# Norm 2 of an encoder layer: four differences go from GpSimd to VectorE, and VectorE's block gets an order of its own

## The chip, the core and the metric

The kernel runs on one core of a Trainium2 chip. The metric is the time of one execution on the device in microseconds. TensorE (PE in the profile) multiplies, VectorE (DVE), ScalarE (ACT) and GpSimd (POOL) work on elements, SyncE (SP) issues the transfers. Each engine works off its own queue in order; semaphores tie the queues together.

## The reference

One encoder layer on 1024 positions of 1024 features, in float32. This is the part that matters here, the second half of the layer:

```python
def rmsnorm(x, g):
    y = x32 * lax.rsqrt(jnp.mean(x32 * x32, axis=-1, keepdims=True) + RMS_EPS)
    return (y * g.astype(jnp.float32)).astype(x.dtype)
...
x = x + gate1 * (merged @ w_out[i])
h2 = rmsnorm(x, g_ffn[i]) * (1 + scale2) + shift2
u = depthwise_conv_seq(h2 @ w_up[i], conv_w[i], conv_b[i])
u_val, u_gate = jnp.split(u, 2, axis=-1)
x = x + gate2 * ((jax.nn.gelu(u_gate, approximate=True) * u_val) @ w_down[i])
```

Before it come the projections, two kinds of attention and the gates; after it a last norm. `w_up` has 1024 x 5632 elements.

## The kernel before

**Precision.** Every product of float32 matrices is three matmuls of a reduced type: each operand is split into a rounded part and the rest (`hi` by ScalarE, `lo = x - hi` by VectorE or GpSimd), and high x high, high x low and low x high are added up in one PSUM bank (lines 948 to 950 for the products of this stage).

**Seven products for eight.** `h2 @ w_up` is done in 22 tiles of 128 columns of each of the two halves of u. Each tile is one 2 x 2 block product by a scheme of seven block products: the weights give the operands 11, S2, S1, S3, 12, S4 and 22, the data give B11, T2, T1, T3, B21, B22 and T4. Positions fall into two halves, features into rows of 128. With B11 and B21 the first four and last four feature rows of half 0 of h2, B12 and B22 those of half 1, the data operands are T3 = B22 - B12, T2 = B11 + T3, T1 = B22 - T2 and T4 = B21 - T2, four rows of 128 x 512 each. They are made once, at norm 2, and serve all 22 tiles.

**The norm 2 block.** `m1[0..7]` are the rows of half 0 (tiles `big` in the profile), scaled and split long before. `m2[0..7]` are those of half 1 (`x` in the profile, x_8576, x_8612, x_8650, x_8688 for 0 to 3 and x_8730, x_8769, x_8808, x_8849 for 4 to 7 in the queues). As soon as the rows come out of the w_out product, `m2[k]` for k < 4 is replaced by the difference `m2[k+4] - m2[k]`: GpSimd makes the first three (line 1123), VectorE the last (line 1129). The reciprocal root of the mean square (`rs`: VectorE line 98, ScalarE line 99, VectorE line 100) is spread over the partitions by TensorE into the PSUM bank `pbc` (line 106). Then VectorE scales the eight rows with it (line 1210), makes `t2[0..3]` = T2 (line 1212; tiles `big` and `wc`) and T1 (line 1214, into `big`). `shifted` (1068 on ScalarE, 1069 on VectorE) adds the shift and splits T2, T3 and B22; `operand` (894 on ScalarE, 895) splits T1 on VectorE and T4 on GpSimd. GpSimd makes T4 (line 1221) between its weight splits (line 56).

**Orders.** Most of the program is put in order by a scheduler that models times. Within the block a written order holds on ScalarE, VectorE and GpSimd, and TensorE's order is as written from the last w_out product to the end of the block. TensorE begins tiles 0 and 1 before the norm is there, with B11 and B21, and goes on with T2, T1, T3, B22 and T4 as they come. What drains the banks of a tile are lines 954 (ScalarE), 956, 958, 961, 966 and 970 (VectorE), the convolution lines 1138 (ScalarE) and 1144 (VectorE), then 1170 (gelu) and 1171. `a_operands` prepares the weights of the next tile: GpSimd 912 to 914, VectorE 921, and splits whose `hi` is ScalarE's line 55 (`whi`, `wsh`, `big`) and whose `lo` is GpSimd's line 56 (`wlo`, `wsl`, `big`). Loads of `w_up` (line 1096, into `wraw` and `big`) start when the tile they fill comes free.

Of the kernel before, what the change touches and what calls it, by code (L numbers as in the profile page):

```python
# [12 lines left out]
OP = mybir.AluOpType  # L13
# [15 lines left out]
def hybrid_encoder(tc, xT, c, w_ada, small, w_in, p1_bias, p23_bias, na_bias, ln2_mult, ident, w_br, w_out,  # L29
                   w_up, w_down, out):  # L30
    nc = tc.nc
    act, dve, pool, pe, sp = nc.scalar, nc.vector, nc.gpsimd, nc.tensor, nc.sync
# [5 lines left out]
    def f(ap):  # L38
        return ap.bitcast(FT)
# [56 lines left out]
    def rstd_of(pcol, n):  # L96
        r = wpool.tile([128, KT], FT, name="rs", bufs=2)
        dve.tensor_scalar(r[:, :n], pcol[:, :n], 1.0 / D, EPS, OP.mult, OP.add)
        act.activation(r[:, :n], r[:, :n], AF.Sqrt)
        dve.reciprocal(r[:, :n], r[:, :n])  # L100
        return r

    def bcast(r, psum_pool, tag, n=4):
        pb = psum_pool.tile([128, 512], FT, name="pbc", tag=tag)
        for t in range(n):
            pe.transpose(pb[:, t * 128:(t + 1) * 128], r[:, t:t + 1].to_broadcast([128, 128]), idt)
        return pb
# [688 lines left out]
    def half_tile(dtype=FT):  # L796
        return mxpool.tile([128, 512], dtype, name="x2", bufs=16)
# [95 lines left out]
    def operand(t, hi, lo, lo_eng):  # L893
        act.activation(hi, t, AF.Copy)
        lo_eng.tensor_tensor(lo, t, f(hi), OP.subtract)
# [85 lines left out]
    def wide(dtype=FT):  # L981
        return keep.tile([128, 512], dtype, name="wc", bufs=5)

    def big(shape, dtype=FT):
        return keep.tile(shape, dtype, name="big", bufs=9)
# [81 lines left out]
    def shifted(src, b, hi, lo):  # L1067
        act.activation(hi, src, AF.Identity, bias=b)
        dve.scalar_tensor_tensor(lo, src, b, f(hi), OP.add, OP.subtract)

    def out_tile(hf, m, sqa, scaled):

        cols = halves[hf]
        w = out_w.pop()
        if hf + m < KT:
            out_w.append(w_split(w_load(w_out[(m + 1) % KT]), pool))
        p = ps.tile([128, 512], FT, name="pj", bufs=6)
        product(p, w, lambda k: [t[:, k, cols] for t in ms])
        xx = x2[hf][m]
        dve.scalar_tensor_tensor(xx, p, ada[:, 16 + m:17 + m], xx, OP.mult, OP.add)  # L1080
        sp.dma_start(x_scr[m][:, cols], xx)
# [19 lines left out]
    m1 = [raw[k // 2][:, k % 2] for k in range(KT)]  # L1101
# [7 lines left out]
    bc = bcast(rstd_of(pcol, 4), ps, "pbc")  # L1109
# [5 lines left out]
    m2 = []  # L1115
# [10 lines left out]
    late_mm.enter_context(tc.manual_schedule(engines={pe.engine}))  # L1126
    m2.append(half_tile())
    sq = out_tile(1, KT - 1, sqa, m2[KT - 1])
    dve.tensor_tensor(m2[3], m2[7], m2[3], OP.subtract)
    mpool.release()  # L1130
    oppool2 = tc.alloc_tile_pool(name="ops2", bufs=1, side="right", reuse_waits="tile")
    for n in ("T2", "T1", "T3"):
# [3 lines left out]
    with tc.tile_pool(name="up", bufs=2, reuse_waits="tile") as work:  # L1136
# [58 lines left out]
        bc = bcast(rstd_of(pcol, 4), ps, "pbc")  # L1195
# [4 lines left out]
        t2 = big([128, 2, 512])  # L1200
        t2 = [t2[:, 0], t2[:, 1], wide(), wide()]

        def t_split(n, k, src, b):
            shifted(src, b, ops[n][0][:, k], ops[n][1][:, k])

        with tc.manual_schedule(engines={act.engine, dve.engine, pool.engine}):

            for k in range(10):
                if k < 8:
                    dve.tensor_tensor(m2[k], m2[k], bc, OP.mult)  # L1210
                if 1 <= k < 5:
                    dve.tensor_tensor(t2[k - 1], m2[k - 1], m1[k - 1], OP.add)
                elif k >= 5 and k < 9:
                    dve.tensor_tensor(m1[k - 5], m2[k - 1], t2[k - 5], OP.subtract)  # L1214
                if 2 <= k < 6:
                    t_split("T2", k - 2, t2[k - 2], shift2[:, 2 + k:3 + k])
                elif k >= 6:
                    operand(m1[k - 6], ops["T1"][0][:, k - 6], ops["T1"][1][:, k - 6], dve)
            for k in range(4):
                t_split("T3", k, m2[k], dshift[:, k:k + 1])  # L1220
                pool.tensor_tensor(m1[4 + k], m1[4 + k], t2[k], OP.subtract)
            for k in range(4):
                late["B22"].append((half_tile(FR), half_tile(FR)))
                shifted(m2[4 + k], shift2[:, 4 + k:5 + k], *late["B22"][k])
            for k in range(4):
                late["T4"].append((half_tile(FR), half_tile(FR)))
                operand(m1[4 + k], *late["T4"][k], pool)
        for g in gens:
# [81 lines left out]
    with tc.manual_schedule(engines={dve.engine}):  # L1310
# [28 lines left out]
        hf, cs, bc = before  # L1339
# [118 lines left out]
```

## Time and profile before

| | |
|---|---|
| three runs | 1565.9, 1569.3 and 1570.37 us; median 1569.3 us |
| the profiled execution | 1566.2 us; its span 1564.4 us; mean granted clock 0.982 |
| busy | PE 96%, PEld 83%, DVE 65%, ACT 52%, POOL 51% |
| the norm 2 block | about 884 to 925 us of the span |
| the 22 tiles of w_up | about 881 us to 1320 us |

A row of the timeline gives the start and the length in microseconds, the engine, the line, the operation, what it writes and reads, and in brackets how long the engine had stood idle before and which engine ended that. The length of a row counts from when the engine took the instruction up, so time in which it is held up by something other than a semaphore is in its length. Rows that follow each other on one line are merged, with a count.

### The profile page before, as it was taken

How to read it: one execution, taken by the hardware profiler on the slowest of the kernel's cores; microseconds unless marked ns; L12 is line 12 of the kernel's file. 1: busy time of each engine (PE TensorE's matmuls, PEld its weight loads, DVE VectorE, ACT ScalarE, POOL GpSimd, SP SyncE). 2: the span in 40 equal slices, each digit the busy share in tenths (PEclk: the TensorE clock that was granted, in tenths of full speed). 3: DMA queues.
4: the chain of work that ended last, by engine and by line, in shares of the span. 5: the costliest groups of instructions: out<-in, count | busy, mean ns of one | idle time of the engine just before them, and what ended most of it. 6: DMA issues, size and time to landing. Idle time of an engine off the chain costs nothing. (4 is left out here: it accounts for less than half of the span.)

```text
span 1564.4 us, 22094 instructions
## 1 busy us (share of the span) xinstructions
PE 1509.5 (96%) x8012; PEld 1291.5 (83%) x8012; DVE 1024.4 (65%) x1874; ACT 805.8 (52%) x1448; POOL 801.8 (51%) x500
## 2 busy tenths in 40 slices
PE   8999799999999999999999888999999999999998
PEld 7899788888887998888888767888888887788787
DVE  6686266676756665535625888766666667877775
ACT  4432366666766677643335454444444446575542
POOL 1242243444337566411256858666666665679621
PEclk9899899999999999999999999999999999999999
DMA  9458522223133453557734212322222223533313
GB/s 352 164 201 292 156 73 73 81 77 93 51 90 111 141 138 104 184 187 238 228 128 149 74 54 81 108 81 81 81 82 90 86 74 136 182 114 121 115 54 109
DMA packets 114421, 196.87 MB, mean 126 GB/s; under 512 B 40200, under 2 KB 61576, under 8 KB 114312
## 3 DMA queue, kind: packets, MB, share of 16 engines
q1 hardware_dynamic: 114040, 195.20, 38.0%
q8 instruction: 63, 1.03, 0.3%
q14 instruction: 46, 0.38, 0.1%
q10 hardware_dynamic: 272, 0.26, 0.1%
HBM read 158.73 MB, written 42.47 MB: 129 GB/s over the span
## 5 line engine op out<-in xcount | busy, mean ns | idle before, releaser
L56 POOL TENSOR_TENSOR wlo<-wraw,whi 128x1024 fp32r<-128x1024 f32 (+2 forms) x78 | 179.9, 2307 | 284.1 <-ACT whi L55 275.1
L79 PE MATMUL pj<-h,whi 128*128 128x512 f32 x448 | 180.5, 403 | 3.8 <-ACT h L202 2.2
L80 PE MATMUL pj<-h,whi 128*128 128x512 f32 x448 | 179.4, 400 | 0.3 <-DVE h L204 0.3
L81 PE MATMUL pj<-h,wlo 128*128 128x512 f32 x448 | 178.8, 399 | 0.0
L56 POOL TENSOR_TENSOR wsl<-big,wsh 128x1024 fp32r<-128x1024 f32 (+1 forms) x45 | 109.3, 2432 | 50.6 <-ACT wsh L55 50.6
L1144 DVE SCALAR_TENSOR_TENSOR big<-wc,sm,big 128x256 f32<-128x256 f32 (+1 forms) x132 | 115.0, 919 | 17.3 <-ACT big L1138 17.2
L55 ACT ACTIVATE whi<-wraw 128x1024 fp32r<-128x1024 f32 (+2 forms) x81 | 81.3, 1003 | 87.0 <-PE pj L80 25.9
L338 POOL TENSOR_SCALAR kl<-kl 64x512 fp32r<-64x512 f32 x32 | 63.8, 1994 | 80.4 <-DVE kl L336 78.1
L79 PEld LDWEIGHTS pj<-h,whi 128*128 128x128 f32 x448 | 85.3, 190 | 20.6 <-ACT ks L337 3.4
L80 PEld LDWEIGHTS pj<-h,whi 128*128 128x128 f32 x448 | 85.4, 191 | 15.9 <-DVE h L204 1.1
L81 PEld LDWEIGHTS pj<-h,wlo 128*128 128x128 f32 x448 | 85.2, 190 | 15.0
L575 DVE CUSTOM_DVE_ANT_0 P<-S,bias 128x256 f32<-128x256 f32 x128 | 52.3, 420 | 53.7 <-PE S L622 31.9
L576 ACT ACTIVATE P<-P,st 128x256 f32<-128x256 f32 x128 | 64.3, 503 | 39.3 <-DVE st L575 38.7
L1144 DVE SCALAR_TENSOR_TENSOR big<-pj,sm,big 128x512 f32<-128x512 f32 x132 | 67.9, 564 | 16.1 <-ACT big L1138 16.1
L56 POOL TENSOR_TENSOR wsl<-wraw,wsh 128x768 fp32r<-128x768 f32 (+1 forms) x23 | 50.1, 2178 | 47.7 <-ACT wsh L55 47.7
L1138 ACT ACTIVATE big<-wc,sm 128x512 f32<-128x512 f32 x44 | 35.8, 816 | 74.5 <-DVE wc L961 45.6
L239 PE MATMUL pv<-vwh,h 128*128 128x256 f32 x256 | 73.7, 288 | 0.4 <-ACT vs L246 0.4
L240 PE MATMUL pv<-vwl,h 128*128 128x256 f32 x256 | 72.5, 283 | 0.0
L241 PE MATMUL pv<-vwh,h 128*128 128x256 f32 x256 | 72.5, 283 | 0.0
L527 POOL TENSOR_TENSOR vv<-vv 96x256 fp32r<-96x256 f32 (+2 forms) x32 | 41.0, 1294 | 59.3 <-ACT vv L526 59.1
L55 ACT ACTIVATE wsh<-big 128x1024 fp32r<-128x1024 f32 (+1 forms) x45 | 44.9, 1002 | 35.4 <-POOL big L913 18.3
L1170 ACT ACTIVATE big<-big 128x1024 f32<-128x1024 f32 x22 | 23.3, 1060 | 76.6 <-DVE big L1144 76.6
(379 smaller groups left out, 4923.7 us busy)
## 6 DMA issues: line engine op xcount, KB each, us to landing
wraw<-w_in SPq DMA_DIRECT2D x36, 512.0 KB, 3.5
wada<-w_ada SPq DMA_DIRECT2D x31, 512.0 KB, 7.1
big<-w_up SPq DMA_DIRECT2D x22, 512.0 KB, 5.0
wraw<-w_up SPq DMA_DIRECT2D x22, 512.0 KB, 3.7
as<-big SPq DMA_DIRECT2D x22, 512.0 KB, 3.0
big<-as SPq DMA_DIRECT2D x22, 512.0 KB, 8.1
wraw<-w_down SPq DMA_DIRECT2D x24, 384.0 KB, 4.2
gs<-gs SPq DMA_DIRECT2D x32, 256.0 KB, 2.5
```

The costliest lines, as they stand in the source:

```text
L55: act.activation(hi, raw, AF.Copy)
L56: lo_eng.tensor_tensor(lo, raw, f(hi), OP.subtract)
L79: pe.matmul(psum, whi[:, k0 + k], mhi, start=k == 0, stop=False)
L80: pe.matmul(psum, whi[:, k0 + k], mlo, start=False, stop=False)
L81: pe.matmul(psum, wlo[:, k0 + k], mhi, start=False, stop=k == n - 1)
L239: pe.matmul(p, hhi, hi[:, k], start=fresh and k == 0, stop=False, skip_group_check=True)
L240: pe.matmul(p, hhi, lo[:, k], start=False, stop=False, skip_group_check=True)
L241: pe.matmul(p, hlo, hi[:, k], start=False, stop=k == KT - 1, skip_group_check=True)
L338: pool.tensor_scalar(ll[b], f(ll[a]), 1.0, None, OP.mult)
L575: dve.tensor_tensor_reduce(pp, d, bias, -1.0, BIG, OP.add, OP.min, mi)
L576: act.activation(pp, pp, AF.Exp, bias=mi, scale=-1.0, accum_out=li)
L1144: dve.scalar_tensor_tensor(y[:, dst], src, wt, y[:, dst], OP.mult, OP.add)
```

## The change

The fourth difference of `m2` no longer stands ahead of the reciprocal. It is made inside the block, of rows 3 and 7 that have both been scaled, where before the difference of the unscaled rows was scaled afterwards. The loop of the block is written out in an order of its own. The four differences of T4 go from GpSimd, where they stood beside the T3 splits, to VectorE, after the splits of B22 and each just ahead of its own T4 split.

```diff
     sq = out_tile(1, KT - 1, sqa, m2[KT - 1])
-    dve.tensor_tensor(m2[3], m2[7], m2[3], OP.subtract)
...
-            for k in range(10):
-                if k < 8:
-                    dve.tensor_tensor(m2[k], m2[k], bc, OP.mult)
-                if 1 <= k < 5:
-                    dve.tensor_tensor(t2[k - 1], m2[k - 1], m1[k - 1], OP.add)
-                elif k >= 5 and k < 9:
-                    dve.tensor_tensor(m1[k - 5], m2[k - 1], t2[k - 5], OP.subtract)
-                if 2 <= k < 6:
-                    t_split("T2", k - 2, t2[k - 2], shift2[:, 2 + k:3 + k])
-                elif k >= 6:
-                    operand(m1[k - 6], ops["T1"][0][:, k - 6], ops["T1"][1][:, k - 6], dve)
...
+            scale(0)
+            scale(1)
+            t2_sum(0)
+            scale(2)
+            t2_sum(1)
+            t2_split(0)
+            scale(7)
+            scale(3)
+            t2_split(1)
+            t2_sum(2)
+            dve.tensor_tensor(m2[3], m2[7], m2[3], OP.subtract)
+            t2_split(2)
+            t2_sum(3)
+            scale(4)
+            t2_split(3)
+            t1_sum(0)
...
             for k in range(4):
                 t_split("T3", k, m2[k], dshift[:, k:k + 1])
-                pool.tensor_tensor(m1[4 + k], m1[4 + k], t2[k], OP.subtract)
...
             for k in range(4):
+                dve.tensor_tensor(m1[4 + k], m1[4 + k], t2[k], OP.subtract)
                 late["T4"].append((half_tile(FR), half_tile(FR)))
                 operand(m1[4 + k], *late["T4"][k], pool)
```

`scale`, `t2_sum`, `t1_sum` and the two splits are the same operations as in the loop, given names. Lines move: scaling is line 1208, T2's sums 1211, T1's 1217, the moved difference 1231, T4's differences 1252; from the convolution to the gelu lines are one lower (1137, 1143, 1169).

VectorE's queue at the start of the block, before (pcol and rs are the sums and the reciprocal root, pbc the spread of it):

```order
L98 TENSOR_SCALAR rs<-pcol 128x4
L1129 TENSOR_TENSOR x_8688<-x_8849,x_8688 128x512
L100 RECIPROCAL rs<-rs 128x4
L1210 TENSOR_TENSOR x_8576<-x_8576,pbc 128x512
L1210 TENSOR_TENSOR x_8612<-x_8612,pbc 128x512
L1212 TENSOR_TENSOR big<-x_8576,big 128x512
L1210 TENSOR_TENSOR x_8650<-x_8650,pbc 128x512
L1212 TENSOR_TENSOR big<-x_8612,big 128x512
L1069 SCALAR_TENSOR_TENSOR T2lo<-big,ada,T2hi 128x512
L1210 TENSOR_TENSOR x_8688<-x_8688,pbc 128x512
```

and the same place now:

```order
L98 TENSOR_SCALAR rs<-pcol 128x4
L100 RECIPROCAL rs<-rs 128x4
L1208 TENSOR_TENSOR x_8576<-x_8576,pbc 128x512
L1208 TENSOR_TENSOR x_8612<-x_8612,pbc 128x512
L1211 TENSOR_TENSOR big<-x_8576,big 128x512
L1208 TENSOR_TENSOR x_8650<-x_8650,pbc 128x512
L1211 TENSOR_TENSOR big<-x_8612,big 128x512
L1069 SCALAR_TENSOR_TENSOR T2lo<-big,ada,T2hi 128x512
L1208 TENSOR_TENSOR x_8849<-x_8849,pbc 128x512
L1208 TENSOR_TENSOR x_8688<-x_8688,pbc 128x512
L1069 SCALAR_TENSOR_TENSOR T2lo<-big,ada,T2hi 128x512
L1211 TENSOR_TENSOR wc<-x_8650,big 128x512
```

The difference of rows 3 and 7 (x_8688, x_8849) no longer stands between line 98 and the reciprocal; row 7 is scaled among the first rows instead of last.

VectorE's queue at the end of the block, before (x_9053 to x_9065 are the low parts of B22):

```order
L1069 SCALAR_TENSOR_TENSOR x_9053<-x_8730,ada,x_9052 128x512
L1069 SCALAR_TENSOR_TENSOR x_9057<-x_8769,ada,x_9056 128x512
L958 TENSOR_TENSOR wc<-pj,wc 128x512
L1069 SCALAR_TENSOR_TENSOR x_9061<-x_8808,ada,x_9060 128x512
L958 TENSOR_TENSOR wc<-pj,wc 128x512
L1069 SCALAR_TENSOR_TENSOR x_9065<-x_8849,ada,x_9064 128x512
L961 TENSOR_TENSOR wc<-pj,wc 128x512
```

and now (the low parts of B22 are x_9049 to x_9061):

```order
L1069 SCALAR_TENSOR_TENSOR x_9049<-x_8730,ada,x_9048 128x512
L1069 SCALAR_TENSOR_TENSOR x_9053<-x_8769,ada,x_9052 128x512
L958 TENSOR_TENSOR wc<-pj,wc 128x512
L1069 SCALAR_TENSOR_TENSOR x_9057<-x_8808,ada,x_9056 128x512
L1069 SCALAR_TENSOR_TENSOR x_9061<-x_8849,ada,x_9060 128x512
L1252 TENSOR_TENSOR big<-big 128x512 x2
L1252 TENSOR_TENSOR big<-big,wc 128x512 x2
L961 TENSOR_TENSOR wc<-pj,wc 128x512
L958 TENSOR_TENSOR wc<-pj,wc 128x512
```

The four differences stand ahead of line 961 of tile 0 and line 958 of tile 1, which drain banks. On GpSimd the four rows of line 1221 that stood between the three `wsl` splits and the split of `big` are gone and nothing takes their place.

TensorE's queue at the first products of tile 2, before:

```order
L948 MATMUL pj<-B21hi,whi 128x512
L949 MATMUL pj<-B21lo,whi 128x512
L950 MATMUL pj<-B21hi,wlo 128x512
L948 MATMUL pj<-T2hi,wsh 128x512
L949 MATMUL pj<-T2lo,wsh 128x512
L948 MATMUL pj<-T1hi,wsh 128x512
L949 MATMUL pj<-T1lo,wsh 128x512
L948 MATMUL pj<-T3hi,wsh 128x512
```

and now:

```order
L948 MATMUL pj<-B11hi,whi 128x512
L949 MATMUL pj<-B11lo,whi 128x512
L950 MATMUL pj<-B11hi,wlo 128x512
L948 MATMUL pj<-T2hi,wsh 128x512
L949 MATMUL pj<-T2lo,wsh 128x512
L948 MATMUL pj<-T1hi,wsh 128x512
L949 MATMUL pj<-T1lo,wsh 128x512
L948 MATMUL pj<-B21hi,whi 128x512
```

The scheduler now puts tile 2's first T2 and T1 matmuls ahead of its twelve B21 matmuls; T3's come after those as before. The orders of tiles 0 to 4 differ in such places, up to where tile 5's first matmuls stand; from there to the end of w_up the products of both kernels stand in the same order.

More of the change, by code (lines that the diff above doesn't have):

```diff
@@ L1206, in hybrid_encoder, with scale, t2_sum, t2_split @@
         with tc.manual_schedule(engines={act.engine, dve.engine, pool.engine}):
-            for k in range(10):
-                if k < 8:
-                    dve.tensor_tensor(m2[k], m2[k], bc, OP.mult)
-                if 1 <= k < 5:
-                    dve.tensor_tensor(t2[k - 1], m2[k - 1], m1[k - 1], OP.add)
-                elif k >= 5 and k < 9:
-                    dve.tensor_tensor(m1[k - 5], m2[k - 1], t2[k - 5], OP.subtract)
-                if 2 <= k < 6:
-                    t_split("T2", k - 2, t2[k - 2], shift2[:, 2 + k:3 + k])
-                elif k >= 6:
-                    operand(m1[k - 6], ops["T1"][0][:, k - 6], ops["T1"][1][:, k - 6], dve)
+            def scale(k):
+                dve.tensor_tensor(m2[k], m2[k], bc, OP.mult)
+            def t2_sum(k):
+                dve.tensor_tensor(t2[k], m2[k], m1[k], OP.add)
+            def t2_split(k):
+                t_split("T2", k, t2[k], shift2[:, 4 + k:5 + k])
+            def t1_sum(k):
+                dve.tensor_tensor(m1[k], m2[4 + k], t2[k], OP.subtract)
+            def t1_split(k):
+                operand(m1[k], ops["T1"][0][:, k], ops["T1"][1][:, k], dve)
+            scale(0)
[14 more added lines that the diff above has]
+            t1_sum(0)
+            scale(5)
+            t1_sum(1)
+            t1_split(0)
+            scale(6)
+            t1_split(1)
+            t1_sum(2)
+            t1_sum(3)
+            t1_split(2)
+            t1_split(3)
             for k in range(4):
                 t_split("T3", k, m2[k], dshift[:, k:k + 1])
-                pool.tensor_tensor(m1[4 + k], m1[4 + k], t2[k], OP.subtract)
             for k in range(4):
```

## The prediction, made before the changed kernel was run

> **What bounds the kernel now.** I read the page first, then TensorE's timeline around norm 2, the table by stretches, then the timelines of the three other engines there.
>
> ```profile
> PE 1509.5 (96%) x8012; PEld 1291.5 (83%) x8012; DVE 1024.4 (65%) x1874; ACT 805.8 (52%) x1448; POOL 801.8 (51%) x500
> 887.01 0.62 PE L106 MATMUL pbc<-idt,rs 128*128 128x128 f32 x4 [4.27 <-DVE rs L100]
> 902.22 0.51 PE L949 MATMUL pj<-T2lo,wsh 128*128 128x512 f32 x1 [2.41 <-DVE T2lo L1069]
> 910.39 0.50 PE L949 MATMUL pj<-T1lo,wsh 128*128 128x512 f32 x1 [3.01 <-DVE T1lo L895]
> 951.60 0.50 PE L948 MATMUL pj<-B21hi,whi 128*128 128x512 f32 x1 [2.65 <-ACT wc L954]
> 975.30 0.50 PE L948 MATMUL pj<-x,big 128*128 128x512 f32 x1 [1.81 <-DVE wc L958]
> ```
>
> TensorE bounds the kernel. Between 880 and 1000 us it stands still for over 1 us five times, 14.15 us in all, and these are the only stalls the change can reach: three wait for VectorE inside the block, two come after it, in tiles 3 and 4.
>
> ```profile
> 880.00:890.00 10.00, 5.73 (x26) 4.48 (x26) 9.11 (x10) 3.41 (x6) 10.00 (x5) 0.89 0.03 10
> 900.00:910.00 10.00, 5.17 (x21) 3.79 (x21) 10.00 (x12) 3.67 (x6) 4.28 (x2) 1.00 0.15 52
> 910.00:920.00 10.00, 9.61 (x35) 7.76 (x36) 8.96 (x12) 7.33 (x12) 3.13 (x2) 0.83 0.01 2
> 920.00:930.00 10.00, 10.00 (x46) 8.28 (x45) 6.71 (x12) 2.12 (x3) 8.99 (x7) 1.00 0.44 157
> 950.00:960.00 10.00, 8.40 (x30) 6.77 (x31) 6.67 (x7) 7.61 (x10) 7.43 (x3) 0.83 0.48 159
> 970.00:980.00 10.00, 8.19 (x30) 6.24 (x29) 7.75 (x8) 3.54 (x5) 6.94 (x5) 0.83 0.20 63
> ...
> 888.79 0.63 PE L949 MATMUL pj<-B11lo,whi 128*128 128x512 f32 x1
> 889.22 0.63 PE L950 MATMUL pj<-B11hi,wlo 128*128 128x512 f32 x1
> ...
> 893.41 0.39 PE L949 MATMUL pj<-B21lo,whi 128*128 128x512 f32 x1
> 893.64 0.39 PE L950 MATMUL pj<-B21hi,wlo 128*128 128x512 f32 x1
> ```
>
> The third figure from the end is the granted clock. A share of 0.83 over 10 us is 3.4 us at half speed. There matmuls follow each other every 0.43 us instead of 0.23, so a half-clock stretch costs 3.4 x (1 - 0.23/0.43) = 1.6 us. Four of the five stalls brought one, the one of 2.41 us (900 to 910, clock 1.00) did not.
>
> **VectorE's chain through the block.**
>
> ```profile
> 883.95 0.15 DVE L98 TENSOR_SCALAR rs<-pcol 128x4 f32<-128x4 f32 x1
> 884.02 2.75 DVE L1129 TENSOR_TENSOR x<-x,x 128x512 f32<-128x512 f32 x1
> 886.70 0.16 DVE L100 RECIPROCAL rs<-rs 128x4 f32<-128x4 f32 x1
> 887.67 1.29 DVE L1210 TENSOR_TENSOR x<-x,pbc 128x512 f32<-128x512 f32 x2 [0.80 <-PE pbc L106]
> ...
> 890.07 2.27 DVE L1212 TENSOR_TENSOR big<-x,big 128x512 f32<-128x512 f32 x1
> 892.26 1.79 DVE L1069 SCALAR_TENSOR_TENSOR T2lo<-big,ada,T2hi 128x512 fp32r<-128x512 f32 x1
> ...
> 898.05 0.74 DVE L1069 SCALAR_TENSOR_TENSOR T2lo<-wc,ada,T2hi 128x512 fp32r<-128x512 f32 x1
> 898.71 0.68 DVE L1210 TENSOR_TENSOR x<-x,pbc 128x512 f32<-128x512 f32 x1
> ...
> 900.41 1.75 DVE L1069 SCALAR_TENSOR_TENSOR T2lo<-wc,ada,T2hi 128x512 fp32r<-128x512 f32 x1
> ...
> 906.28 2.85 DVE L1214 TENSOR_TENSOR big<-x,wc 128x512 f32<-128x512 f32 x1
> ...
> 909.66 1.28 DVE L895 TENSOR_TENSOR T1lo<-big,T1hi 128x512 fp32r<-128x512 f32 x2
> 884.13 0.20 ACT L99 ACTIVATE rs<-rs 128x4 f32<-128x4 f32 x1 [1.82 <-DVE rs L98]
> 883.44 8.35 POOL L56 TENSOR_TENSOR wsl<-big,wsh 128x1024 fp32r<-128x1024 f32 x3
> 891.75 3.45 POOL L1221 TENSOR_TENSOR big<-big 128x512 f32<-128x512 f32 x2
> 899.89 1.72 POOL L56 TENSOR_TENSOR big<-wraw,big 128x512 fp32r<-128x512 f32 x1
> 905.92 2.67 POOL L56 TENSOR_TENSOR wlo<-wraw,whi 128x1024 fp32r<-128x1024 f32 x1 [4.30 <-ACT whi L55]
> ```
>
> A pass that reads one operand from PSUM takes 0.60 us (two in 1.29, the second 0.69 long) whatever GpSimd does. One that reads two from SBUF takes the same when GpSimd is idle, but ends only 0.6 us after a running GpSimd instruction does: the sum at 890.07 ends at 892.34, the three `wsl` splits at 891.79. So VectorE queues behind GpSimd instruction by instruction. Three splits less two VectorE passes of 0.6 that got in between, from 884.0 to 891.79, make 2.2 us a split. A T2 low part costs 0.66 (898.05 to 898.71).
>
> **The change, step by step.** *The difference ahead of the reciprocal.* The root is there at 884.33; the reciprocal comes at 886.70, since L1129 stood behind a `wsl` split. Without it the reciprocal starts at about 884.4: 2.3 us earlier, and TensorE's first stall shrinks from 4.27 to 1.95. Scaling begins at 885.35.
>
> *GpSimd takes most of that back.* The first T2 sum, at 886.55, meets the second split (886.2 to 888.4) and ends at 889.0. The second waits out the third split and ends at 891.8, 0.5 us ahead of before.
>
> *The four differences leave GpSimd.* The first low part of T2 then need not wait for line 1221 (892.26, 1.79 long): it ends at 892.5 instead of 894.05. Two scalings and the second low part: 894.35.
>
> ```profile
> 896.42 0.76 ACT L1138 ACTIVATE big<-pj,sm 128x512 f32<-128x512 f32 x1
> 897.08 0.62 ACT L55 ACTIVATE big<-wraw 128x512 fp32r<-128x512 f32 x1
> 898.16 0.72 ACT L1068 ACTIVATE T2hi<-wc,ada 128x512 fp32r<-128x512 f32 x1 [0.46 <-DVE wc L1212]
> 904.78 1.06 ACT L55 ACTIVATE whi<-wraw 128x1024 fp32r<-128x1024 f32 x1 [0.75 <-DMA wraw<-w_up]
> 901.64 18.30 SPq L1096 DMA_DIRECT2D wraw<-w_up  x2
> ```
>
> ScalarE now does the convolution and the split of `big` (0.76 and 0.62) right after the second T2 high part, at 892.5, so GpSimd's split of `big` gets in behind the second low part, 894.35 to 895.6, and holds up the third T2 sum to 896.2. The moved difference (0.6) to 896.8, then the low part once its high part (0.72) is there, 897.7; the fourth sum and one scaling; the last low part ends at 899.75 against 902.16. The load of `w_up` is issued when that split ends, 895.6 instead of 901.6, and lands 3.1 us later (901.64 to 904.78); ScalarE takes it at 899.05, and GpSimd's `wlo` split holds the port from 900.35 to 902.55, where it held it at 906.28 before. It costs VectorE one wait of 1 us, not 2.2: the second T1 sum ends at 903.15. Seven passes of 0.6 later, at 907.4, stands the third low part of T1, for which TensorE waited before (909.66 + 0.68 = 910.34). **TensorE is then 2.9 us ahead.** If the `wlo` split held up two passes, not one, it would be 1.9; if none, 3.9.
>
> *The differences on VectorE.* Four passes, 2.4 us, more where one meets a T4 split. VectorE is 6.71 busy of 10 between 920 and 930, which hides them from TensorE's T4 products. But they stand ahead of lines 961, 958 and 966, and ScalarE's convolution and the weight splits of tile 2 stand behind those.
>
> ```profile
> 937.54 1.04 ACT L55 ACTIVATE wsh<-wraw 128x1024 fp32r<-128x1024 f32 x1
> ...
> 938.74 0.40 PE L948 MATMUL pj<-T3hi,wsh 128*128 128x512 f32 x1
> ```
>
> Before, that split of tile 2 was done at 938.58, 0.16 us ahead of its first use. With TensorE 2.9 us ahead and ScalarE held by 2.4 us of differences, the split comes 0.5 us ahead of before, and TensorE waits there for 2.9 - 0.16 - 0.5 = 2.2 us. Bounds: 0 (the differences fit into VectorE's idle time) and 5 (they don't, and a T4 split is waited for twice).
>
> *The later stalls.* Those at 951.60 and 975.30 hang on the drain of tiles 2 and 3, whose order is new too. I take them as they are, 4.46 us, give or take 1.5. The few swaps in the w_down stage I cost at nothing, give or take 1: no stall of the block reaches them.
>
> *The clock.* TensorE's waits become more and shorter. By the rows, 1.81 us is enough for a half-clock stretch and 2.41 may do without, so I count half a stretch fewer than the four: -0.8; bounds -3.2 and +1.6. The Trainium skill (TensorE: Matmul & The Clock Gate, Part 1) lets the clock fall only after an idle window of about 3.4 us; by that the 4.27 us stall alone was charged, and with 1.95 us its 1.6 us would go for certain. The trace disagrees: 0.83 at 970 to 980 follows a stall of 1.81.
>
> **The sum.** -2.9 + 2.2 + 0 - 0.8 = -1.5 us. The profiled execution took 1566.2 us (span 1564.4 and 1.8 around it) and lies at the low end of the runs (1565.9 to 1570.37); set against the median of 1569.3 it gives **1567.8 us**, 0.1% less. A measurement of this kernel can tell about 0.3%, 4.7 us, from no change.
>
> **Rivals.** *VectorE becomes the bound behind the block* (slower). The four differences, each behind a GpSimd instruction, put the drains of tiles 0 and 1 so late that tile 2's splits come later than the 937.54 of before; that is the point from which it decides. TensorE then waits the whole 2.9 in tile 2 and the 2.4 of the differences on top, and two more half-clock stretches come: -2.9 + 5.3 + 3.2 = +5.6, 1574.9 us. For it: VectorE is 8.96 and 10.00 busy of 10 just before. Against it: 6.71 after, with idle time before the drains.
>
> *The whole advance is kept* (faster). Tile 2 does not wait, since ScalarE's splits come as early as TensorE, and two half-clock stretches go: -2.9 - 3.2 = -6.1, 1563.2 us. For it: the head stall of 1.95 and a broken T1 wait may both keep the clock. Against it: the slack of 0.16 us before that split's use.
>
> *The moved difference gains nothing* (no change): GpSimd's three splits end at the same time either way and T2's sums wait for them. Then 0.5 us of the advance is left, and with the tile 2 wait gone too and the clock as it is, -0.5: 1568.8 us. It shares its class with the forecast.
>
> **Chances.** Forecast 0.50 and no gain 0.14, both within 0.3%: 0.64. Whole advance kept 0.20, VectorE the bound 0.16. The range is 1563.0 to 1574.0: the forecast with the bounds of the T1 wait, the tile 2 wait and the clock, into the edge of both rivals, about 1 in 10 left out on each side.
>
> **What would show it.** In the profile after: the reciprocal within 0.5 us of the root, and a first stall near 2 us; the first two T2 sums still long, ending with the `wsl` splits; T2's last and T1's third low part 15.8 and 23.5 us after the start of line 98 (before, 18.2 and 26.4); a new stall of TensorE of 1 to 3 us before tile 2's T3, ended by ScalarE's `wsh`; three or four stretches at half clock between 880 and 1000. The prediction is wrong if T1's low part is not ahead, if tile 2's stall is absent or above 4 us, or if the time moves by more than 4.7 us either way.

## The result, and the profile after

The changed kernel takes 1568.6 us in the median of 14 runs (1565.27 to 1572.66), the kernel before 1569.84 us (14 runs, 1565.65 to 1573.73). The ratio is 0.9995, 95% interval 0.9983 to 1.0006: no change that can be told. 1567.8 us was predicted. The profiled execution took 1570.64 us, its span 1568.8 us, at a mean granted clock of 0.977. Line 98 of norm 2 starts at 889.46 us in it, at 883.95 before; what came earlier is the same program, so below "after line 98" means after that start in the same profile.

TensorE's timeline of the changed kernel (start, length, what it does, in brackets the wait and what ended it):

```profile
890.20 0.62 PE L106 MATMUL pbc<-idt,rs 128*128 128x128 f32 x4 [1.95 <-DVE rs L100]
902.51 0.50 PE L948 MATMUL pj<-T2hi,wsh 128*128 128x512 f32 x1 [1.70 <-ACT T2hi L1068]
913.23 0.51 PE L948 MATMUL pj<-T1hi,wsh 128*128 128x512 f32 x1 [0.66 <-ACT T1hi L894]
926.70 0.47 PE L948 MATMUL pj<-x,wsh 128*128 128x512 f32 x1 [0.45 <-ACT x L894]
938.17 0.50 PE L948 MATMUL pj<-T2hi,wsh 128*128 128x512 f32 x1 [0.30 <-ACT wsh L55]
955.26 0.80 PE L948 MATMUL pj<-T2hi,wsh 128*128 128x512 f32 x1 [2.97 <-ACT wsh L55]
958.96 0.79 PE L948 MATMUL pj<-x,big 128*128 128x512 f32 x1 [1.56 <-DVE wc L958]
980.02 0.47 PE L948 MATMUL pj<-x,big 128*128 128x512 f32 x1 [0.72 <-DVE wc L958]
```

The three stalls of the block, 4.27, 2.41 and 3.01 us, have become 1.95, 1.70 and several of 0.2 to 0.7. Behind the block it is the other way round: tile 3 now waits 2.97 and 1.56 us where one wait of 2.65 stood, tile 4 waits 0.72 instead of 1.81, and T4's product (926.70) waits 0.45 us for ScalarE, which waits for the moved differences. The table by stretches (the third figure from the end is the granted clock) shows five half-clock stretches of 3.4 us, two at 900 to 910 and three at 950 to 970, where before had four:

```profile
900.00:910.00 10.00, 7.64 (x17) 4.75 (x18) 9.50 (x14) 3.65 (x5) 3.76 (x2) 0.68 0.15 52
940.00:950.00 10.00, 10.00 (x45) 8.06 (x44) 9.96 (x9) 3.86 (x5) 10.00 (x6) 1.00 0.28 93
950.00:960.00 10.00, 5.47 (x18) 3.41 (x17) 8.42 (x8) 4.64 (x6) 6.88 (x4) 0.74 0.54 177
960.00:970.00 10.00, 10.00 (x35) 8.05 (x34) 7.10 (x10) 2.68 (x5) 8.04 (x6) 0.75 0.12 47
```

VectorE's timeline through the block:

```profile
889.46 0.15 DVE L98 TENSOR_SCALAR rs<-pcol 128x4 f32<-128x4 f32 x1
889.88 0.18 DVE L100 RECIPROCAL rs<-rs 128x4 f32<-128x4 f32 x1 [0.27 <-ACT rs L99]
892.06 2.61 DVE L1211 TENSOR_TENSOR big<-x,big 128x512 f32<-128x512 f32 x1
895.19 2.31 DVE L1211 TENSOR_TENSOR big<-x,big 128x512 f32<-128x512 f32 x1
897.42 0.74 DVE L1069 SCALAR_TENSOR_TENSOR T2lo<-big,ada,T2hi 128x512 fp32r<-128x512 f32 x1
904.64 0.75 DVE L1069 SCALAR_TENSOR_TENSOR T2lo<-wc,ada,T2hi 128x512 fp32r<-128x512 f32 x1 [0.19 <-ACT T2hi L1068]
907.31 1.47 DVE L1217 TENSOR_TENSOR big<-x,big 128x512 f32<-128x512 f32 x1
911.23 0.69 DVE L956 TENSOR_TENSOR wc<-pj,wc 128x512 f32<-128x512 f32 x1 [0.64 <-PE pj L950]
913.21 1.30 DVE L895 TENSOR_TENSOR T1lo<-big,T1hi 128x512 fp32r<-128x512 f32 x2
922.36 1.28 DVE L1252 TENSOR_TENSOR big<-big 128x512 f32<-128x512 f32 x2
923.57 2.38 DVE L1252 TENSOR_TENSOR big<-big,wc 128x512 f32<-128x512 f32 x2
933.35 0.69 DVE L970 TENSOR_TENSOR wc<-pj,wc 128x512 f32<-128x512 f32 x1 [0.63 <-PE pj L950]
```

The reciprocal follows the root at once; the first two T2 sums wait out GpSimd's splits (2.61 and 2.31 us); the last T2 low part is done 15.8 us after line 98. At 911.23 VectorE waits for TensorE, which ran at half clock until 0.9 us before that (granted clock 0.68 from 900 to 910 us, 0.98 from 910 to 920). The four T4 differences take 3.6 us from 922.36 on; by 933.35, at the drain of the last product, VectorE is waiting for TensorE again.

Behind the block stands the place that the prediction missed. GpSimd, VectorE and ScalarE of the changed kernel at tiles 2 and 3:

```profile
939.97 2.87 POOL L56 TENSOR_TENSOR wsl<-big,wsh 128x1024 fp32r<-128x1024 f32 x1
942.79 2.29 POOL L912 TENSOR_TENSOR big<-big 128x512 f32<-128x512 f32 x1
945.04 2.57 POOL L56 TENSOR_TENSOR wsl<-wraw,wsh 128x1024 fp32r<-128x1024 f32 x1
949.00 1.74 POOL L913 TENSOR_TENSOR big<-big 128x512 f32<-128x512 f32 x1
...
943.84 9.28 DVE L1143 SCALAR_TENSOR_TENSOR big<-wc,sm,big 128x255 f32<-128x255 f32 x6
...
940.88 1.04 ACT L55 ACTIVATE wsh<-wraw 128x1024 fp32r<-128x1024 f32 x1
953.21 1.06 ACT L1169 ACTIVATE big<-big 128x1024 f32<-128x1024 f32 x1 [9.34 <-DVE big L1143]
954.17 1.04 ACT L55 ACTIVATE wsh<-big 128x1024 fp32r<-128x1024 f32 x1
```

Six convolution passes take 9.28 us: five of them end 0.3 to 0.55 us after the GpSimd instruction beside them does, and the sixth takes 0.47; ScalarE's gelu waits 9.34 us for them, the `wsh` split of tile 3 stands behind the gelu, and TensorE's 2.97 us at 955.26 is that split. The kernel before has the same row, a tenth of a per cent shorter, and the same wait of ScalarE:

```profile
940.64 9.27 DVE L1144 SCALAR_TENSOR_TENSOR big<-wc,sm,big 128x256 f32<-128x256 f32 x6
950.01 1.06 ACT L1170 ACTIVATE big<-big 128x1024 f32<-128x1024 f32 x1 [9.49 <-DVE big L1144]
```

**TensorE's lost time.** At full clock the products' matmuls (lines 948 to 950) start every 0.2275 us. I add up what each start-to-start distance has above that, from 5 us ahead of line 98 to 35 us after it (the block), and from there to 110 us after (the tiles behind it). A distance that is 0.12 to 0.28 us too long is counted as half clock, the rest as waiting. All profiles of this study, in us, with the ratio of the times (the labels are those of the experiments below):

| kernel | block: waiting, half clock | behind: waiting, half clock | sum | time against before, 95% |
|---|---|---|---|---|
| before | 12.39, 3.10 | 5.37, 2.91 | 23.8 | |
| before_again | 12.37, 3.13 | 5.25, 3.03 | 23.8 | 1.0005 (0.9996 to 1.0015) |
| changed | 9.45, 2.45 | 8.26, 2.99 | 23.2 | 0.9995 (0.9983 to 1.0006) |
| after_again | 9.40, 1.52 | 9.15, 1.59 | 21.7 | 1.0003 (0.9990 to 1.0017) |
| head_only | 9.66, 4.38 | 5.52, 1.19 | 20.7 | 1.0011 (0.9996 to 1.0026) |
| t4_only | 8.97, 1.39 | 7.17, 1.19 | 18.7 | 0.9996 (0.9984 to 1.0008) |
| order_only | 13.42, 2.67 | 6.13, 1.39 | 23.6 | 1.0015 (1.0003 to 1.0028) |
| head_t4 | 9.15, 1.68 | 8.12, 0.00 | 18.9 | 0.9999 (0.9986 to 1.0011) |
| no_splits | 8.73, 2.54 | 8.26, 2.02 | 21.5 | 1.0006 (0.9991 to 1.0021) |
| t4_triple | 9.54, 1.39 | 14.54, 5.52 | 31.0 | 1.0082 (1.0068 to 1.0096) |
| after_prep | 9.68, 1.96 | 9.14, 2.53 | 23.3 | 1.0010 (1.0001 to 1.0020) |
| headt4_prep | 9.42, 1.38 | 7.79, 3.15 | 21.7 | 0.9996 (0.9983 to 1.0009) |
| before_prep | 12.29, 1.73 | 9.03, 1.53 | 24.6 | 1.0003 (0.9991 to 1.0014) |
| no_late_splits | 9.49, 1.00 | 0.72, 0.00 | 11.2 | 0.9911 (0.9894 to 0.9928) |

The block waits 2.9 to 3.0 us less in the changed kernel, and the tiles behind it wait 2.9 to 3.9 us more. Two executions of one kernel differ by up to 0.8 us in all their waiting and by up to 2.3 us at half clock; smaller differences say little.

### The profile page after: what moved, and what is told of

Same layout as the page of the kernel before. It is cut to its first block, busy times and chain, and to the rows that moved or that the text cites. A ratio compares the mean times of both kernels' runs of the same rounds, so it can differ in the third digit from the quotient of the medians.

```text
span 1568.8 us, 22098 instructions
## 1 busy us (share of the span) xinstructions
PE 1515.4 (97%) x8012; PEld 1293.5 (82%) x8012; DVE 1028.2 (66%) x1878; ACT 806.3 (51%) x1448; POOL 794.4 (51%) x496
## 5 line engine op out<-in xcount | busy, mean ns | idle before, releaser
L1143 DVE SCALAR_TENSOR_TENSOR big<-wc,sm,big 128x256 f32<-128x256 f32 (+1 forms) x132 | 118.0, 942 | 17.3 <-ACT big L1137 17.2
L1169 ACT ACTIVATE big<-big 128x1024 f32<-128x1024 f32 x22 | 23.3, 1061 | 78.3 <-DVE big L1143 78.3
```

The lines of the kernel that those rows point to most:

```text
L1143: dve.scalar_tensor_tensor(y[:, dst], src, wt, y[:, dst], OP.mult, OP.add)
```

## The experiments

My theory when these began: the block's gain is real and is handed back behind the block. The rivals: the loss behind it is an accident of one execution; one of the two edits makes the gain and the other costs; VectorE has become the bound.

**The same kernels again.** Two runs without an edit.

> The changed kernel once more, for what a second profile of it shows. TensorE's progress is read as the time from the start of line 98 at norm 2 to its 50th, 150th, 200th, 250th, 300th and 400th matmul after the spread of the root. In the first pair of profiles the changed kernel stood at -1.45, -2.89, -2.16, +2.12, +2.10 and -0.64 us against the kernel before. Theory (stalls are fixed by the order, the clock is not): the stalls come back within 0.3 us each, the 150th stands at -2.9, give or take 1.6, and the loss between the 200th and the 250th comes back by the stalls of 2.97 and 1.56 us, with the half-clock stretches there one to three. Rival (the loss of 4.3 us between the 200th and the 250th is an accident of one execution): the two stalls there are gone or below 1 us. Time: within 0.2% of the kernel before by both.

TensorE's timeline behind the block, of after_again:

```profile
936.79 0.50 PE L948 MATMUL pj<-T2hi,wsh 128*128 128x512 f32 x1 [0.30 <-ACT wsh L55]
941.99 0.50 PE L948 MATMUL pj<-T3hi,wsh 128*128 128x512 f32 x1 [1.24 <-ACT wsh L55]
954.13 0.50 PE L948 MATMUL pj<-T2hi,wsh 128*128 128x512 f32 x1 [1.85 <-ACT wsh L55]
957.84 0.80 PE L948 MATMUL pj<-x,big 128*128 128x512 f32 x1 [1.63 <-DVE wc L958]
```

The 150th matmul stands at -3.60 us, the 200th at -1.50, the 250th at +0.83, the 400th at -1.86: the loss behind the block is no accident. But the stalls are not fixed to 0.3 us: the 1.70 us before T2 is 0.47 here, tile 2's T3 waits 1.24 us where it did not wait, tile 3 waits 1.85 instead of 2.97. With one half-clock stretch fewer in the block and one fewer behind it (three against five by the granted clock from 5 us ahead of line 98 to 105 after it) TensorE arrives 0.7 us earlier at tile 2 and waits there instead.

> The kernel before once more, for a second profile. Theory (waits are set by the order, half-clock stretches fall by chance): the five stalls come back, 4.27, 2.41, 3.01, 2.65 and 1.81 us, within 0.4 each; between 5 us ahead of line 98 and 105 us after it the clock loses 3.4 to 8.5 us (two to five stretches; 6.9 in the first profile), and the 400th matmul after the spread comes at 112.2, give or take 2. Rival (the stretches follow the stalls): again four stretches at the same four stalls, and the 400th at 112.2, give or take 0.5.

The 400th matmul came at 112.24 us (112.22), the half-clock stretches at the same four stalls. The rival held: two executions of before are alike to 0.03 us.

**The edits one by one.** In the kernel before, the difference is moved to the scaling of row 3, nothing else:

```diff
-    dve.tensor_tensor(m2[3], m2[7], m2[3], OP.subtract)
...
             for k in range(10):
+                if k == 3:
+                    dve.tensor_tensor(m2[3], m2[7], m2[3], OP.subtract)
                 if k < 8:
```

> The kernel before with one edit: the difference of rows 3 and 7 stands just ahead of the scaling of row 3 instead of ahead of the reciprocal; order and T4 as before. Theory (the head gain is lost to GpSimd without the second part): the spread of the root comes 2.3 us earlier, but T2's first low part still waits for the three wsl splits and then for line 1221, so the 150th matmul is at 0 to -1 us and the 400th at 0, give or take 1.6; time within 0.1% of before. Rival (the moved difference is the whole gain, T4's move costs): the 150th at -2.3 us and kept through the 400th; time -0.15%.

TensorE's long waits in the block, but for the first, from its timeline:

```profile
900.55 0.50 PE L949 MATMUL pj<-T2lo,wsh 128*128 128x512 f32 x1 [1.33 <-DVE T2lo L1069]
903.92 0.80 PE L949 MATMUL pj<-T2lo,wsh 128*128 128x512 f32 x1 [2.40 <-DVE T2lo L1069]
906.27 0.80 PE L949 MATMUL pj<-T2lo,wsh 128*128 128x512 f32 x1 [0.70 <-DVE T2lo L1069]
```

The 150th matmul stands at -1.20 us, the 400th at -2.78. Both theories miss: T2's low parts do make TensorE wait 4.43 us in three places, but no T1 stall is left, and the block waits 2.7 us less than before. What hides this at the 150th is 1.3 us more at half clock. Behind the block nothing of it is handed back in waiting: 5.52 us there, 5.37 before.

The other edit alone, in the loop order of before:

```diff
-                pool.tensor_tensor(m1[4 + k], m1[4 + k], t2[k], OP.subtract)
...
             for k in range(4):
+                dve.tensor_tensor(m1[4 + k], m1[4 + k], t2[k], OP.subtract)
                 late["T4"].append((half_tile(FR), half_tile(FR)))
```

> The kernel before with the other edit alone: the four T4 differences on VectorE at the end of the block; the fourth difference of the unscaled rows stays ahead of the reciprocal. Theory: the spread comes as before (+3.1 us after line 98), the first T2 low part no longer waits for line 1221, so the 150th matmul is at -1 to -2 us; behind the block tile 3's order is that of the changed kernel, so 2 to 4 us are lost between the 200th and the 250th; the 400th at 0 to +2, time 0 to +0.15%. Rival (VectorE's load at the end of the block costs nothing): the 250th stands where the 150th does, the 400th at -1 to -2, time -0.1%.

TensorE's timeline of it, three of its waits:

```profile
889.18 0.62 PE L106 MATMUL pbc<-idt,rs 128*128 128x128 f32 x4 [4.23 <-DVE rs L100]
907.55 0.51 PE L949 MATMUL pj<-T1lo,wsh 128*128 128x512 f32 x1 [1.56 <-DVE T1lo L895]
...
938.11 0.80 PE L948 MATMUL pj<-T3hi,wsh 128*128 128x512 f32 x1 [3.93 <-ACT wsh L55]
```

More than expected: the 150th at -4.16 us, since T2 no longer waits at all. Then tile 2's T3 waits 3.93 us for ScalarE's `wsh`: this is the stall the prediction had expected of the changed kernel, nearly twice as long. The 400th stands at -4.77, but only because two half-clock stretches are left; in waiting alone, 16.1 against 17.8 us, the gain is 1.6 us, and the time moved by -0.04%. Up to the end of w_up the lead stays (-4.8 us at the 1800th product), but 2.2 us of it are gone by the last product, in the w_down stage.

Both edits together, still in the loop order of before:

> The kernel before with both edits in its own loop order: the difference of rows 3 and 7 just ahead of the scaling of row 3, and the four T4 differences on VectorE; the block's new order is left out. Theory (the gains of the two edits overlap, since GpSimd's three splits hold T2's sums in either, and the new order costs): the spread at +0.74 us, the 150th at -4 to -5 us against before, so 1 us and more ahead of the changed kernel; tile 2's T3 waits 3 to 4.5 us for ScalarE's wsh split as with the T4 edit alone, and the 400th stands at -4 to -5. Rival (the gains add up): the 150th at -6 or further. Second rival (the new order is needed for the head gain): the 150th at -3 or less. Time: within 0.2% of before by all.

The 150th stands at -3.71 us, the 400th at -4.57; the block's waiting is 9.15 us. Single gains of 2.7 and 3.4 us give 3.2 together: they overlap, as the theory had it, though the 150th is not as far ahead as the 4 to 5 us that I had put. Tile 2's T3 waits 2.04 us, less than expected. By the distances over 0.28 us, T4's product and tile 3 lose 0.6 and 3.5 us, where before lost nothing and 2.8, and tile 4 loses 1.1 instead of 2.0. The lead at the 400th is nearly all clock: in waiting alone, 17.3 against 17.8 us, the gain is 0.5 us; by the last product 1.7 us of the lead are gone too.

And the changed kernel with T4's differences back on GpSimd, so that the new order and the scaled difference stand alone:

```diff
                 t_split("T3", k, m2[k], dshift[:, k:k + 1])
+                pool.tensor_tensor(m1[4 + k], m1[4 + k], t2[k], OP.subtract)
...
-                dve.tensor_tensor(m1[4 + k], m1[4 + k], t2[k], OP.subtract)
```

> The changed kernel with the four T4 differences back on GpSimd, one behind each split of T3, as before; the new order and the scaled difference stay. Theory: the spread comes at +0.75 us as in the changed kernel, but T2's first low part waits for GpSimd's first difference, so the 150th matmul is about 1 us less ahead than in the changed kernel (-1 to -2); the loss between the 200th and the 250th is smaller, since VectorE is freed of 2.4 us; time within 0.1% of before. Rival (the order alone makes the gain): the 150th at -2.9 and the 250th at -1 to -3, time -0.15%.

Neither. The block waits 13.42 us, 1.0 more than before and 3.8 more than head_only, which has the same early reciprocal; the 150th stands at +0.85 and the time is 0.15% longer (0.03 to 0.28). So the new order alone costs; with T4's differences moved it is neither gain nor loss (9.45 and 9.40 against 9.15).

This run also bears on the tiles behind the block. TensorE's timeline of it, at tile 3:

```profile
955.27 0.72 PE L948 MATMUL pj<-T2hi,wsh 128*128 128x512 f32 x1 [2.99 <-ACT wsh L55]
958.98 0.80 PE L948 MATMUL pj<-x,big 128*128 128x512 f32 x1 [1.57 <-DVE wc L958]
```

These are the two stalls of the changed kernel (2.97 and 1.56 us), in a kernel that is not ahead and has T4's differences on GpSimd. It loses 6.1 us at tile 3, where before lost 2.8, and nothing at tile 4, where before lost 2.0. The second stall goes with the scheduler's order: in both kernels VectorE's line 921, 2.3 us long beside a GpSimd split, stands ahead of line 958, for which TensorE waits (956.04 and 958.23 us in the changed kernel), and in before it stands behind it (953.63 and 953.03). In head_only the products of w_up stand as in before, and tile 3 waits 2.69 us, once. So the new order behind the block is a rival to the account that an advance is handed back there, and by these rows it accounts for tile 3's second stall. It does not account for all: order_only waits 6.13 us behind the block, 0.8 more than before, and the changed kernel 8.26 and 9.15. No kernel here has both edits and before's order in these tiles, so the shares were not separated.

**What holds the block.** The changed kernel without the three splits that GpSimd does at the head of the block; these weights' low parts are replaced by their high parts:

```diff
+            if names in bare:
+                act.activation(hi, src, AF.Copy)
+                lo = hi
+            else:
+                split(src, hi, lo, eng)
...
```

> The changed kernel without the low parts of the three wsl splits that GpSimd does at the head of the block (tile 0's S2/S1 and S3/22, tile 1's S2/S1; TensorE multiplies by the high part once more instead, so the products of those weights are rough). Theory (these three splits hold the first two T2 sums): the sums take 0.7 us each instead of 2.61 and 2.31, VectorE is some 3 us further at T2, TensorE's waits between 11 and 35 us after line 98 halve, and the 150th matmul comes 2 to 3 us earlier than in the changed kernel (-5 to -6.5 us against before). Tile 2's wsh split does not follow by as much, so 1 to 3 us of it go to a wait there. Rival (ScalarE's high parts and the half-clock TensorE pace T2 anyway): the 150th within 1 us of the changed kernel's.

VectorE's timeline (its lines are four higher here):

```profile
893.40 0.69 DVE L1215 TENSOR_TENSOR big<-x,big 128x512 f32<-128x512 f32 x1
894.60 0.69 DVE L1215 TENSOR_TENSOR big<-x,big 128x512 f32<-128x512 f32 x1
897.83 0.75 DVE L1073 SCALAR_TENSOR_TENSOR T2lo<-big,ada,T2hi 128x512 fp32r<-128x512 f32 x1 [0.69 <-ACT T2hi L1072]
901.29 1.27 DVE L1073 SCALAR_TENSOR_TENSOR T2lo<-wc,ada,T2hi 128x512 fp32r<-128x512 f32 x1 [1.51 <-ACT T2hi L1072]
```

The sums shrink to 0.69 us as expected, and it hardly helps: VectorE waits for ScalarE's high parts next, the block's waiting falls by 0.7 us only, the 150th matmul (-3.65 us) stands where after_again has it (-3.60). By this number the rival held. Its reason holds in part: T2's last low part is done 13.8 us after line 98, 2.0 us earlier than in the changed kernel, so T2 is not held as long; but T1's second low part then takes 2.87 us beside GpSimd's `wlo` split, and T1's third is done at 22.9 us, only 0.8 and 1.5 us ahead of the changed kernel's two profiles.

**What holds the tiles behind it.** The changed kernel with each T4 difference done three times:

```diff
+                late["T4"].append((half_tile(FR), half_tile(FR)))
+                for _ in range(2):
+                    dve.tensor_tensor(late["T4"][k][1], m1[4 + k], t2[k], OP.subtract)
                 dve.tensor_tensor(m1[4 + k], m1[4 + k], t2[k], OP.subtract)
-                late["T4"].append((half_tile(FR), half_tile(FR)))
```

> The changed kernel with each of the four T4 differences on VectorE done three times (the first two into the tile of T4's low part, which is overwritten): eight passes more. Theory (VectorE has no room left behind the block, the drains and ScalarE's splits hang on it): up to the 150th matmul nothing changes; tile 2's wsh split for S3 comes 4 to 6 us later than in the changed kernel and TensorE waits about as long ahead of tile 2's T3, so the 200th stands 3 to 6 us behind the changed kernel; time +0.2 to +0.4%. Rival (the drains have idle time to spare): the 200th within 1 us of the changed kernel, time within 0.1%.

TensorE's timeline of it, at T4's products (x) and at tile 2:

```profile
922.67 0.50 PE L949 MATMUL pj<-x,wsh 128*128 128x512 f32 x1 [0.67 <-POOL x L895]
924.66 0.75 PE L948 MATMUL pj<-x,wsh 128*128 128x512 f32 x1 [1.26 <-ACT x L894]
945.08 0.69 PE L948 MATMUL pj<-T2hi,wsh 128*128 128x512 f32 x1 [3.25 <-ACT wsh L55]
948.39 0.80 PE L948 MATMUL pj<-T3hi,wsh 128*128 128x512 f32 x1 [1.34 <-ACT wsh L55]
```

Eight passes more, five of 0.6 us and three of about 1.1 beside a T4 split of GpSimd, some 6 us of VectorE, make the kernel 0.82% slower, 12.9 us, where I had expected 0.2 to 0.4%. The tiles behind the block lose 8.8 and 9.3 us more than in the two profiles of the changed kernel; the profiled execution, the fastest of its five, took 1577.92 us, 7.3 more than theirs. T4's products now wait for their operands too, tile 2 waits 4.6 us, and half clock behind the block takes 5.5 us instead of 3.0 and 1.6. So the prediction's slower rival, VectorE as the bound, sets in somewhere within these eight passes; the products of tiles 2 to 4 stand in another order here too.

Next, ScalarE's splits: tile 2's weights are prepared a tile earlier in the program, so that both its `wsh` splits stand ahead of tile 0's gelu on ScalarE. In the changed kernel, in head_t4 (headt4_prep), and in before:

```diff
+                if t == 0 and j == 5:
+                    prep2 = a_operands(raw.pop(2), 4, lambda t: work, sts[2])
+                    for _ in range(3):
+                        next(prep2)
...
```

> The changed kernel with tile 2's weights prepared one tile earlier in the program: three of its four steps are given right after tile 1's last step, ahead of tile 0's drains, so that on ScalarE tile 2's two wsh splits stand ahead of tile 0's gelu and its table load. Theory (what the block gains is handed back because ScalarE splits tile 2's and 3's weights behind the drains and the gelu of tiles 0 and 1): TensorE's lost time between 35 and 82 us after line 98, 10.3 and 9.7 us in the two profiles of the changed kernel and 4.5 in both of before, falls to 6 or less; the 400th matmul stands at -3 to -6 us against before; time -0.1 to -0.3%. Rival (VectorE's drains bound these tiles; ScalarE's splits only show it): the lost time there stays above 8, time within 0.1%.

> Both edits in the loop order of before, with tile 2's weights prepared a tile earlier as in the run beside it. Theory: the lost time between 35 and 82 us, 6.9 us without the early preparation, falls to 4 or less, since tile 2's stall of 2.2 us ahead of T3 goes; the 400th matmul at -5.5 to -8 us; time -0.2 to -0.4%, the best of all. Rival (the drains bound): the stall goes to tile 3, 6 us or more are still lost there, time within 0.1%.

> The kernel before with nothing but tile 2's weights prepared a tile earlier. Theory (the slack of before at tile 2's T3 is enough, its split is not what TensorE waits for, and the early preparation pays only together with a block that is ahead): lost time between 35 and 82 us within 1.5 us of before's 4.5, time within 0.15%. Rival (the early preparation is a gain of its own): lost time there 2 or less, time -0.2%.

VectorE's and TensorE's timelines of after_prep:

```profile
931.20 8.24 DVE L1143 SCALAR_TENSOR_TENSOR big<-wc,sm,big 128x255 f32<-128x255 f32 x5
943.85 4.68 DVE L1143 SCALAR_TENSOR_TENSOR big<-wc,sm,big 128x512 f32<-128x512 f32 x2
...
949.47 0.51 PE L948 MATMUL pj<-T2hi,wsh 128*128 128x512 f32 x1 [4.68 <-DVE big L1143]
```

Tile 2's wait is gone; 4.68 us appear at tile 3, ended by VectorE's convolution, whose passes queue behind the earlier GpSimd splits instead. Waiting behind the block is 9.14 us (8.26 and 9.15 without the early preparation), in headt4_prep 7.79 (8.12), and before_prep loses 3.7 us by it (5.1 us are lost between 35 and 82 us, as the theory had it, but the rest comes later). The 400th matmul stands at -0.47, -1.77 and +1.06 us. The theory that ScalarE's place in the queue costs the gain falls: between 35 and 82 us headt4_prep still loses 7.2 us, as the rival put it, and after_prep 7.5, between the 6 of the theory and the 8 of the rival, and none of the three is faster (after_prep is 0.10% slower, 0.01 to 0.20). The scheduler's orders behind the block differ in all three, so this is not ScalarE's place alone.

Last, the changed kernel without GpSimd's low parts for the weights of tiles 2 and 3 (the high parts stand in for them; the edit is that of no_splits, given for these tiles):

> The changed kernel without GpSimd's low parts of the weights of tiles 2 and 3 (TensorE multiplies by the high part once more instead, so these two tiles are rough); the splits of tiles 0 and 1 and GpSimd's sums of weights stay. Theory (behind the block VectorE has no idle time, and its convolution passes queue behind GpSimd's splits of tiles 2 and 3, which hands the block's gain back): each merged row of line 1143 is shorter, TensorE loses 5 us or less between 35 and 82 us after line 98 (10.3 and 9.7 in the changed kernel, 4.5 before) and the 400th matmul stands at -5 to -7 us against before; time -0.2 to -0.4%. Rival (the drains wait for the order of TensorE and ScalarE, not for GpSimd): the loss there stays at 8 or more and the time within 0.1%.

VectorE's timeline of it (lines four higher), and a row of its table by stretches:

```profile
939.43 1.53 DVE L1147 SCALAR_TENSOR_TENSOR big<-wc,sm,big 128x512 f32<-128x512 f32 x3
941.49 1.13 DVE L1147 SCALAR_TENSOR_TENSOR big<-wc,sm,big 128x512 f32<-128x512 f32 x2
...
950.00:960.00 10.00, 10.00 (x46) 8.25 (x45) 9.19 (x14) 4.38 (x5) 4.82 (x4) 1.00 0.00 0
```

The same convolution passes take 0.5 us each instead of 1.5, TensorE's waiting behind the block falls from 8.3 or 9.2 us to 0.7, no half-clock stretch is left there, the 400th matmul stands at -12.3 us, and the time falls by 0.89% (0.72 to 1.06), 14 us, over twice what I had expected. With the splits out of the way TensorE hardly waits behind the block, so nothing is handed back there; the kernel before without these splits was not run, so how much of the 14 us the change would keep is not shown. The Trainium skill (SBUF — State Buffer, SBUF: two separate sides) says that VectorE and GpSimd share one pair of ports by an exclusive lock held for a whole instruction, which a VectorE operation with two SBUF inputs needs too. The rows agree: passes on `wc` and `big` take 1.5 us each beside running splits and 0.5 without.

Left open: this run also takes GpSimd's splits out of the scheduler's orders, and which part of the 12 us that accounts for was not separated. It leaves work out, so no kernel of this study that computes the layer beats before by more than can be told.

## Why the prediction was right, and where not

*The difference ahead of the reciprocal*: right. First stall 1.95 us, as put.

*GpSimd takes most of that back*: the rows came as put (sums of 2.61 and 2.31, last T2 low part at 15.8 us, the load of `w_up` issued early, one wait of 0.8 us at 907.31 for the `wlo` split). As a cause it was too narrow: without those splits T2 is done 2.0 us earlier, but ScalarE's high parts and GpSimd's next split leave 0.8 to 1.5 us of that at T1.

*TensorE 2.9 us ahead at T1*: right in size. The block waits 2.94 and 2.97 us less, profile against profile. T1's third low part stood 24.4 us after line 98 instead of 23.5, because TensorE had run at half clock and line 956 waited 0.64 us for it; in after_again, without a half-clock stretch there, it stood at 23.7.

*2.2 us given back at tile 2's T3*: the mechanism, TensorE waiting for ScalarE's weight splits, was right in kind, the place and the size were not. This is the step that failed. Tile 2's `wsh` split ended 52.5 and 53.2 us after line 98 (54.6 before), 1.5 to 2.2 us earlier and not 0.5, because the differences fitted into VectorE's idle time and the drains waited for TensorE as before; TensorE waited 0 and 1.24 us there. By the prediction's own sign, tile 2's stall absent, its account of this place is refuted in the first profile. *The later stalls*, taken as unchanged, grew by 1.9 and 1.2 us. By the distances over 0.28 us, tile 3 lost 5.8 and 5.1 us in the two profiles where before lost 2.8, tile 2 0.5 and 1.9 where before lost nothing, tile 4 0.9 where before lost 2.0, and T4's product, where the differences were counted as hidden, 0.6. All waiting behind the block grew by 2.9 and 3.9 us, where 2.2 had been put. The prediction had seen that the order of tiles 2 and 3 was new and still took their stalls as they were; order_only shows that tile 3's two stalls come with that order even without an advance. What the order and the advance each cost stays open.

*The clock, -0.8*: -0.6 and -3.1 us of lost time in the two pairs of profiles, within the bounds. Five stretches came in the first, one more than before, and cost 5.4 us against 6.0, so their number is not their price. The Trainium skill (TensorE: Matmul & The Clock Gate, Part 1) says that the window by which the clock is judged runs freely. By that it would matter where in a window a wait falls, and the traces fit: the wait of 2.41 us had no half-clock stretch in its wake, that of 1.70 two, that of 1.81 one. Waits of 1.70 and 1.81 us were thus enough for a stretch, as the prediction had read from its rows.

*The w_down stage, at nothing*: from the end of w_up to the last product the changed kernel gained 0.7 us on before in the first profile and lost 1.1 in the second, about the bound of 1.

*The sum, -1.5*: lost time -0.6 and -2.1 us in the two profiles, -1.2 in the median times. That the median came so near is luck: the interval of the ratio reaches from -2.7 to +0.9 us, the second set of runs came out at +0.03%, and a forecast of no change would have fitted as well. The gain of the block was foreseen; that as much would be lost behind it, and where, was not.

Of the rivals, *the whole advance kept* was refuted by tile 3, *VectorE the bound* by the tile 2 split, which came earlier than before's; t4_triple shows how near that one was. *The moved difference gains nothing* is refuted by head_only in waiting, while in time it cannot be told from the forecast.

## What to carry to other kernels

A gain inside one stage is worth what the next stage lets through: look for the engine that stays busy behind it (here VectorE, whose two-input passes queue behind GpSimd's weight splits) before pricing the gain. Where a scheduler orders the next stage anew, compare that order too: here a stall behind the block came with it. Two edits that shorten the same chain do not add up: 2.7 and 3.4 us gave 3.2. Compare waiting and half clock apart, since from one execution of the changed kernel to the next waiting changed by 0.8 us and the half-clock part by 2.3.

## What was not expected of the hardware

Six small VectorE passes, 3 us of work, took 9.3 us beside a GpSimd that was idle only in the last 0.9 us of them, in the kernel before as in the changed one. Without GpSimd's splits for two tiles of 22, and with the orders that come of it, the kernel is 14 us shorter.

The time of this kernel goes with its granted clock. In 35 runs of the kernel before, those at a mean clock of 0.982 took 1565.8 to 1568.0 us, those at 0.977 1571.1 to 1574.1; the correlation is -0.76. Both profiles of before were of the first kind (1566.2 and 1566.8 us), so single profiles of two kernels compare draws of the clock as well as programs. A part of the program that no edit touched, 390 to 460 us, ran at a clock of 1.00 in both profiles of before and at 0.98 and 0.95 in those of the changed kernel, which is 1.6 and 2.8 us of the 5 us by which line 98 came later there.
